# One level of Strassen's method for the gate and up products of four feed-forward blocks

## The chip, the cores and the metric

The kernel runs on one core of a Trainium2 chip. The metric is the device time of one execution in microseconds; the median of several executions counts. In what follows PE is the matrix engine, DVE the vector engine, ACT the scalar engine, POOL the engine GpSimd, and SP the queue that issues the transfers.

## The reference, cut to what matters

The model is one inference step of a two-layer decoder trunk over 512 prompt tokens and 64 sample tokens (576 columns together) of width 1024. Each layer has a feed-forward block ahead of its token mixer and another behind its cross attention, so there are four such blocks in all. The hidden width `D_FF` is 2816.

```python
def swiglu(x, w_gu, w_down):
    gate, up = jnp.split(x @ w_gu, 2, axis=-1)
    return (jax.nn.silu(gate) * up) @ w_down

for l in range(DEPTH):
    x = x + 0.5 * swiglu(rmsnorm(x, ffn1_norm[l]), ffn1_w_gu[l], ffn1_w_down[l])
    # token mixer, cross attention
    x = x + 0.5 * swiglu(rmsnorm(x, ffn2_norm[l]), ffn2_w_gu[l], ffn2_w_down[l])
```

All data are 32-bit floats.

## The kernel before, in words

Activations lie transposed: 128 rows of the width on the partitions, the 576 tokens along the free axis, eight such chunks `xT[:, c]`. A product in full precision is made of three products in the faster format fp32r: each operand is split into a rounded high part `h` and a remainder `l`, and PE adds up hh, hl and lh. ACT makes `h` (a cast), DVE makes `l` (a subtraction).

`unit` (line 273) loads 256 columns of a weight, all 1024 rows, as one transfer of 1 MB into a `raw` buffer (two of them), and splits it in two halves of 128x1024 each into `wh` and `wl` (three buffers each; the cast is line 297, the subtraction line 298). `mm3` (line 302) makes 128 rows of the result: 8 chunks of the width, times 3 products, times 2 halves of 288 tokens, which is 48 matmuls of 288 columns into a pair of PSUM banks `psd` (two pairs). So a unit of 256 weight columns takes 96 matmuls.

`ffn` (line 402) walks the 22 hidden chunks in three parts of 8, 8 and 6 chunks. In each part it goes by two chunks at a time: a gate unit and an up unit. DVE multiplies the gate's PSUM by the norm's factor `rstd` (line 420), ACT takes Silu (line 421), DVE multiplies the up's PSUM by `rstd` (line 424) and then by the gate (line 425), and `split` makes the two parts of the hidden chunk (lines 318 and 319). At the end of a part the down product runs over the part's hidden chunks for all eight output chunks, and `add_x` (line 1392) adds each to `xT`. In the last part `nxt` follows each output chunk: `norm_chunk` (line 323) makes the next block's split input `xn` from one chunk of `xT` (lines 333 and 334) and adds its squares to `acc` (lines 348 and 350, on POOL). `norm_finish` (line 397) sums `acc` over the partitions with PE (line 388) and makes `rstd`.

The program is written for a framework that sets all waits itself and that fixes, before the run, the order of the instructions of each engine from the order of the code, the dependencies and the free buffers. On the chip each engine takes its instructions strictly in that order. Tags with a number of buffers hold the chunks: `x0` and `x1` (pairs), `y`, `m`, `g0`, `g1`, `t0`, `t1`.

Of the kernel before, what the change touches and what calls it, by code (L numbers as in the profile page):

```python
# [140 lines left out]
class Net:  # L141
    def __init__(self, ctx, tc, a, o):
        self.tc, self.nc, self.a, self.o = tc, tc.nc, a, o
        sb = lambda n, b: ctx.enter_context(tc.tile_pool(name=n, bufs=b))
        self.cp = sb("const", 1)
        self.wp = sb("weights", 2)
        self.kp = sb("chunks", 1)
        self.sp = sb("small", 4)
        self.dp = ctx.enter_context(tc.tile_pool(name="dram", bufs=1, space=bass.MemoryType.DRAM))
        self.pd = ctx.enter_context(tc.tile_pool(name="pd", bufs=2, space=bass.MemoryType.PSUM))  # L150
        self.pm = ctx.enter_context(tc.tile_pool(name="pm", bufs=4, space=bass.MemoryType.PSUM))
        self.bufs = dict(y=8, m=11, g0=6, g1=6, t0=3, t1=3)
        self.n = 0
        self.tmp = 't'
        self.lane = 0
# [10 lines left out]
    def ct2(self, lane, dt=F32):  # L166
        return self.kp.tile([P, 2, T], dt, tag=f"x{lane}", bufs=4, name=self.nm("x"))

    def tt(self):
        return self.ct(self.tmp)  # L170
# [8 lines left out]

    def psm(self):  # L180
        return self.pm.tile([P, 512], F32, tag=f"m{self.lane}", bufs=2, name=self.nm("pm"))

# [88 lines left out]

    # -- dense products ---------------------------------------------------
    def unit(self, *srcs, ksplit=False):
# [28 lines left out]
    def mm3(self, w, xin):  # L302
# [11 lines left out]
        return ps[:, :, :TH]  # L314

    def split(self, x, tag='y'):
        h, l = self.ct(tag, F32R), self.ct(tag, F32R)
# [5 lines left out]
    def norm_chunk(self, c, name, base, squares=True):  # L323
# [6 lines left out]
        if name != 'final_norm':  # L330
            t = self.ct2(c % 2, F32R)
# [68 lines left out]

    # -- feed forward -----------------------------------------------------
    def ffn(self, l, which, nxt, begin=None, then=None):
        nc = self.nc
        gu, dn = self.a[f'ffn{which}_w_gu'][l], self.a[f'ffn{which}_w_down'][l]
        units = lambda m0: [self.unit(gu[:, c * P:(c + 2) * P]) for c in (m0, KF + m0)]
        first = units(0)
        if begin:
            begin()
        self.norm_finish()
        xn, rstd = self.xn, self.v2(self.rstd)  # L410
        self.tmp = 'g'
        parts = [(0, 8), (8, 16), (16, 22)]
        for pi, (c0, c1) in enumerate(parts):
            hid = []
            for m0 in range(c0, c1, 2):
                ug, uu = units(m0) if m0 else first
                for j in range(2):
                    pg = self.mm3(ug[j], xn)
                    z = self.tt()
                    nc.vector.tensor_mul(self.v2(z), pg, rstd)  # L420
                    nc.scalar.activation(z, z, AF.Silu)
                    pu = self.mm3(uu[j], xn)
                    h = self.tt()
                    nc.vector.tensor_mul(self.v2(h), pu, rstd)  # L424
                    nc.vector.tensor_mul(h, h, z)
                    hid.append(self.split(h, 'y' if len(hid) < 4 else 'm'))
                if then and m0 == 2:
                    then()
# [7 lines left out]

    # -- even mixer -------------------------------------------------------
    def col_scale(self, ps):
# [157 lines left out]
    def even_mixer(self, filler, nxt):  # L596
# [22 lines left out]
        def proj(h):  # L619
            self.lane = h % 2  # L620
            uf, uq = self.unit(col(4, h), col(3, h))
            _, t = self.half_tanh(self.mm3(uf, xn))
            f, k = self.ct('m'), self.ct('m')
            nc.vector.tensor_scalar(f, t, c1[:, h:h + 1], c0[:, h:h + 1], ALU.mult, ALU.add)
# [73 lines left out]

    # -- odd mixer: retention ---------------------------------------------
    def rope(self, ps):  # L700
# [6 lines left out]
        out = self.ct('m')  # L707
        nc.vector.tensor_add(out, t, sw)
        return out
# [25 lines left out]

    # -- odd mixer: delta rule --------------------------------------------
    def shift_mix(self, ps, ci, dst):
# [25 lines left out]
    def prep(self, j, w_in):  # L763
        col = lambda g: w_in[:, 2048 + g * 512 + j * P:2048 + g * 512 + (j + 1) * P]
        ur, uk = self.unit(col(0), col(1))
        uv, = self.unit(col(2))
        tag = 'g' if j < 2 else 'm'
        r, kd, v = self.ct(tag), self.ct(tag), self.ct('m')
        for ci, u, t in ((j, ur, r), (4 + j, uk, kd), (8 + j, uv, v)):
# [311 lines left out]
    def odd_mixer(self, filler, nxt):  # L1081
# [20 lines left out]
        def proj(h):  # L1102
            uq, uk = self.unit(col(0, h), col(1, h))
            q = self.rope(self.mm3(uq, xn))
            k = self.rope(self.mm3(uk, xn))
            uv, ug = self.unit(col(2, h), col(3, h))
# [66 lines left out]

    # -- cross attention --------------------------------------------------
    def mem_stats(self):
# [14 lines left out]

    def wkv(self, l, tag):
        nc, a, o = self.nc, self.a, self.o
# [3 lines left out]
        for c in range(0, KD, 4):  # L1196
# [5 lines left out]
            for k in range(4):  # L1202
                if k % 2 == 0:
                    h, lo = self.ct(tag, F32R), self.ct(tag, F32R)
                ks, g = slice(k % 2 * MEM, (k % 2 + 1) * MEM), self.vec('mem_norm', l * KD + c + k)
# [76 lines left out]
    def xattn(self, l, nxt):  # L1282
# [8 lines left out]
        for m0 in range(0, KD, 2):  # L1291
            u = self.unit(a['xattn_wq'][l][:, m0 * P:(m0 + 2) * P])
            for j in range(2):
                t = self.ct('g')
                nc.vector.tensor_mul(self.v2(t), self.mm3(u[j], self.xn), self.v2(rs))
                nc.gpsimd.tensor_copy(qs[:, m0 + j], t[:, TP:])
                q.append([self.ct('y' if m0 < 4 else 'm', F32R)[:, :TP] for _ in range(2)])
                self.split_to(*q[-1], t[:, :TP])
# [9 lines left out]
        def prompt_head(h):  # L1308
# [17 lines left out]
            for d in range(2):  # L1326
                c = 2 * h + d
                ps = self.psm()
                for m in range(2):
                    for i, k in pairs:  # L1330
                        nc.tensor.matmul(ps, v[m][i][:, c // 4, c % 4 * P:(c % 4 + 1) * P], pT[m][k],  # L1331
                                         start=(m + i + k == 0), stop=(m == 1 and i == 1))
                tag = 'y' if h in (1, 2) else 'm'
                out[c] = self.ct(tag, F32R), self.ct('g1' if c == 1 else tag, F32R)
                self.split_to(*(t[:, :TP] for t in out[c]), ps)
# [90 lines left out]
def network(tc, a, o):  # L1426
    with ExitStack() as ctx:
# [3 lines left out]
        n.ffn(0, 1, after('mix_norm', 0), lambda: n.norm_all('ffn1_norm', 0), n.setup_rest)  # L1431
        n.even_mixer(lambda: n.wkv(0, 'y'), after('xattn_norm', 0))
        n.xattn(0, after('ffn2_norm', 0))
        n.ffn(0, 2, after('ffn1_norm', 1))
        n.ffn(1, 1, after('mix_norm', 1))
        n.odd_mixer(lambda: n.wkv(1, 'y'), after('xattn_norm', 1))
        n.xattn(1, after('ffn2_norm', 1))
        n.ffn(1, 2, after('final_norm', 0))
# [16 lines left out]
```

## Time and profile before

| what | us |
|---|---|
| median of 3 runs | 3076.28 |
| lowest and highest run | 3063.57, 3079.44 |
| span of the profiled execution | 3078.6 |
| PE busy in that span | 3002.7 |
| DVE, ACT, POOL busy in that span | 1480.8, 1006.3, 273.6 |

For the profiled execution no device time is listed beside its span; the span of 3078.6 us runs from its first to its last instruction and lies within the range of the timed runs, 2.3 us over their median. The three runs lie 16 us apart. Busy times are times in which the engine had an instruction in work; that PE is busy for 98% of the span does not say yet that each matmul is needed, only that it hardly waits.

### The profile page before, as it was taken

To read this page: it belongs to the slowest core of one execution; us is meant where nothing else is said; L and a number is where in the kernel's file an instruction comes from. 1 tells how busy PE (TensorE), PEld (TensorE's weight loads), DVE (VectorE), ACT (ScalarE), POOL (GpSimd) and SP (SyncE) were. 2 spreads that over 40 slices of the span, in tenths; PEclk is the share of its full clock that TensorE was granted. 3 is DMA by queue.
4 is the path that set the end of the run, shared out by engine and by line. 5 is a ranking of instruction groups with operands and counts; after the bars stand their busy time and mean duration, and the time that the engine had idled before them with its cause. 6 is when DMAs were issued, how large, how long until landed. Compare 5 with 4: busy or idle time off the path is not lost.

```text
span 3078.6 us, 52891 instructions
## 1 busy us (share of the span) xinstructions
PE 3002.7 (98%) x23236; PEld 2849.9 (93%) x23236; DVE 1480.8 (48%) x2271; ACT 1006.3 (33%) x1495; POOL 273.6 (9%) x299
## 2 busy tenths in 40 slices
PE   8999999999999999999999999999989999999998
PEld 7999999998978999999999999988767788999998
DVE  4434346555545433334434345466576545433333
ACT  4322242222534322224212134433253434322223
POOL 0000011111101000001000001123222100000001
PEclk9999999999999999999999999999889999999999
DMA  4222222222445222222222223322113244222221
GB/s 136 96 84 83 84 77 70 70 84 91 146 174 170 72 84 84 84 80 80 83 83 83 83 83 89 86 63 67 39 43 84 83 162 168 83 83 83 83 79 62
DMA packets 295869, 278.63 MB, mean 91 GB/s; under 512 B 25028, under 2 KB 278808, under 8 KB 295640
## 3 DMA queue, kind: packets, MB, share of 16 engines
q1 hardware_dynamic: 295640, 275.26, 28.2%
q8 instruction: 183, 3.00, 0.4%
q14 instruction: 46, 0.38, 0.0%
HBM read 262.09 MB, written 13.14 MB: 89 GB/s over the span
## 4 chain that ended last, share of the span: by engine, by line
PE 89%; ACT 3%; DVE 3%; issue 2%; POOL 1%; DMA 1%; SPq 0%; ACTq 0%; POOLq 0%; DVEq 0%
PE pd L311 74%; PE pm L833 2%; PE pm L757 1%; PE pd L1222 1%; PE pm L388 1%; PE pd L1253 1%; PE pd L1221 1%; PE pd L1223 1%; PE pm L527 1%; PE pm L1347 1%; PE pm L1315 1%; PE pm L1331 1%; POOL acc L350 1%; PE pm L566 1%; PE pm L942 1%
## 5 line engine op out<-in xcount | busy, mean ns | idle before, releaser
L311 PE MATMUL pd<-x,wh 128*128 128x288 f32 x8000 | 1415.4, 298 | 4.5 <-ACT wh L297 4.3
L311 PEld LDWEIGHTS pd<-x,wh 128*128 128x128 f32 x8000 | 1188.7, 190 | 10.6 <-ACT wh L297 5.4
L311 PE MATMUL pd<-x,wl 128*128 128x288 f32 x4000 | 867.1, 298 | 0.0
L297 ACT CAST wh<-raw 128x1024 fp32r<-128x1024 f32 (+1 forms) x378 | 389.6, 1031 | 1346.9 <-PE pd L311 1252.4
L311 PEld LDWEIGHTS pd<-x,wl 128*128 128x128 f32 x4000 | 649.5, 190 | 2.5 <-DVE wl L298 0.3
L298 DVE TENSOR_TENSOR wl<-raw,wh 128x1024 fp32r<-128x1024 f32 (+1 forms) x378 | 454.9, 1204 | 32.4 <-ACT wh L297 6.8
L311 PE MATMUL pd<-y,wh 128*128 128x288 f32 x2304 | 415.6, 300 | 1.1 <-ACT y L318 0.8
L311 PEld LDWEIGHTS pd<-y,wh 128*128 128x128 f32 x2304 | 343.7, 190 | 5.4 <-ACT y L318 1.1
L1392 DVE SCALAR_TENSOR_TENSOR xT<-pd,xT 128x576 f32<-128x576 f32 x144 | 108.8, 756 | 402.1 <-PE pd L311 402.1
L311 PE MATMUL pd<-m,wh 128*128 128x288 f32 x1504 | 264.0, 296 | 0.3 <-ACT m L1279 0.3
L311 PE MATMUL pd<-y,wl 128*128 128x288 f32 x1152 | 251.6, 299 | 0.0
L424 DVE TENSOR_TENSOR g<-pd,rstd 128x576 f32<-128x576 f32 x88 | 66.6, 756 | 374.6 <-PE pd L311 374.6
L311 PEld LDWEIGHTS pd<-m,wh 128*128 128x128 f32 x1504 | 222.1, 189 | 0.8 <-ACT m L1279 0.8
L311 PEld LDWEIGHTS pd<-y,wl 128*128 128x128 f32 x1152 | 187.7, 190 | 1.4
L350 POOL TENSOR_TENSOR acc<-acc,g 128x576 f32<-128x576 f32 x27 | 41.8, 1550 | 1602.4 <-ACT g L348 1258.1
L311 PE MATMUL pd<-m,wl 128*128 128x288 f32 x768 | 164.4, 296 | 0.0
L420 DVE TENSOR_TENSOR g<-pd,rstd 128x576 f32<-128x576 f32 x88 | 66.6, 756 | 196.2 <-PE pd L311 196.0
L311 PEld LDWEIGHTS pd<-m,wl 128*128 128x128 f32 x768 | 123.8, 189 | 0.0
L1222 PE MATMUL pd<-wh,y 128*128 128x256 f32 x256 | 77.6, 303 | 0.0
L1223 PE MATMUL pd<-wl,y 128*128 128x256 f32 x256 | 77.3, 302 | 0.0
L1221 PE MATMUL pd<-wh,y 128*128 128x256 f32 x256 | 76.3, 298 | 0.6 <-DVE y L1207 0.6
L287 ACT CAST wh<-raw 128x1024 fp32r<-128x1024 f32 x32 | 33.5, 1046 | 121.6 <-PE pd L1222 60.9
(461 smaller groups left out, 2946.3 us busy)
## 6 DMA issues: line engine op xcount, KB each, us to landing
raw<-ffn_w_gu SPq DMA_DIRECT2D x88, 1024.0 KB
raw<-ffn_w_down SPq DMA_DIRECT2D x32, 1024.0 KB
raw<-xattn_wkv SPq DMA_DIRECT2D x16, 1024.0 KB
x<-cache_mem_v SPq DMA_DIRECT2D x32, 512.0 KB
raw<-cache_mem_k SPq DMA_DIRECT2D x16, 1024.0 KB
raw<-odd_w_in SPq DMA_DIRECT2D x30, 512.0 KB
raw<-ffn_w_down SPq DMA_DIRECT2D x16, 768.0 KB
raw<-even_w_in SPq DMA_DIRECT2D x16, 512.0 KB
```

The source lines that it names most:

```text
L287: nc.scalar.copy(h, raw[:, k:k + nk // 2])
L297: nc.scalar.copy(h, raw[:, :, c:c + step])
L298: nc.vector.tensor_sub(l, raw[:, :, c:c + step], h.bitcast(F32))
L311: nc.tensor.matmul(ps[:, hf, :TH], w[:, k], x[:, hf * TH:(hf + 1) * TH], start=(k == 0 and w is wh and xi == 0), stop=(k == nk - 1 and w i ...
L350: eng.tensor_add(self.acc, self.acc, sq)
L420: nc.vector.tensor_mul(self.v2(z), pg, rstd)
L424: nc.vector.tensor_mul(self.v2(h), pu, rstd)
L833: self.nc.tensor.matmul(ps[q, c * 64:(c + 1) * 64], *fn(c, q))
L1221: nc.tensor.matmul(ps[:, m, :256], mh[:, ms], wh, start=(k == 0), stop=False)
L1222: nc.tensor.matmul(ps[:, m, :256], ml[:, ms], wh, start=False, stop=False)
L1223: nc.tensor.matmul(ps[:, m, :256], mh[:, ms], wl, start=False, stop=(k == KD - 1))
L1392: self.nc.vector.scalar_tensor_tensor(x, ps, s, x, ALU.mult, ALU.add)
```

## The change

The gate and up products are made with Strassen's method in the form with seven products. The weight's 1024 rows are taken as two sets (even and odd chunks), its 256 columns as two halves, and the 576 tokens as two halves of 288. Each of the seven products has a combination of weight blocks and a combination of token blocks as its operands, 4 chunks of the width and 3 products of fp32r, so 12 matmuls of 288 columns; seven of them replace the 96 matmuls of a unit by 84.

The combinations of the weight blocks are made on POOL, in place in `raw`: four additions or subtractions of 128x512 for each unit. Each of the seven forms is split by one cast on ACT and one subtraction on DVE of 128x512. The seven results are combined as they leave PSUM: a copy and two additions of 128x288 on DVE (`p1`, `u2`, `u3`), and then one `put` for each quarter of the result. For the gate, three quarters are a DVE addition and a POOL multiplication by `rstd` and one is a DVE multiplication; after Silu, POOL multiplies by `rstd` again for the up product. For the up product, three quarters are a DVE addition and a DVE multiplication and one is a DVE multiplication.

The token blocks' seven combinations are made ahead, in `token_forms`, once for each pair of chunks as the block before delivers it. The parts become 6, 6, 6 and 4 hidden chunks. `y` becomes six pair buffers, which the forms T4, B21 and B22 hold through a block; `m` has 7 buffers in place of 11, and users of `y` and `m` elsewhere are adapted.

```diff
-        self.bufs = dict(y=8, m=11, g0=6, g1=6, t0=3, t1=3)
+        self.bufs = dict(m=7, g0=6, g1=6, t0=3, t1=3)
...
+    def pair(self, dt=F32):
+        return self.kp.tile([P, 2, T], dt, tag="y", bufs=6, name=self.nm("y"))
...
+    def form(self, src, n):
+        nc = self.nc
+        nj = src.shape[1]
+        t = self.wp.tile([P, 1024], F32R, tag=("wh", "wl")[n % 2], bufs=3, name=self.nm("wf"))
+        h, l = (t[:, i * nj * P:(i + 1) * nj * P].rearrange("p (j f) -> p j f", j=nj) for i in range(2))
+        nc.scalar.copy(h, src)
+        nc.vector.tensor_sub(l, src, h.bitcast(F32))
+        return h, l
+
+    def unit_forms(self, *srcs):
...
+        v = raw.rearrange("p (j two) f -> p two j f", two=2)
+        a11, a12, a21, a22 = v[:, 0, :, :P], v[:, 1, :, :P], v[:, 0, :, P:], v[:, 1, :, P:]
+        s3 = self.ct('t1')[:, :nk * 64].rearrange("p (j f) -> p j f", f=P)
+        nc.gpsimd.tensor_sub(s3, a21, a11)
+        nc.gpsimd.tensor_add(a21, a21, a22)
+        yield self.form(a11, 0)
+        nc.gpsimd.tensor_sub(a11, a21, a11)
+        yield self.form(a11, 1)
+        yield self.form(s3, 0)
+        yield self.form(a21, 1)
+        nc.gpsimd.tensor_sub(a11, a12, a11)
+        yield self.form(a22, 0)
+        yield self.form(a11, 1)
+        yield self.form(a12, 0)
...
+    def seven(self, forms, x, put):
+        nc = self.nc
+        w = lambda: next(forms)
+        ps = self.psd()
+        a, d = ps[:, 0, :TH], ps[:, 1, :TH]
+        s, s_ = self.v2(self.ct('t0')), self.ct('t0')
+        p1, u2, u3 = s[:, 0], s[:, 1], s_[:, :TH]
+        self.product(a, w(), x['B11'])
+        nc.vector.tensor_copy(p1, a)
+        b = self.psm(0)[:, :TH]
+        self.product(b, w(), x['T2'])
+        nc.vector.tensor_add(u2, b, p1)
+        c = self.psm(1)[:, :TH]
+        self.product(c, w(), x['T3'])
+        nc.vector.tensor_add(u3, c, u2)
+        self.product(d, w(), x['T1'])
+        put(1, 1, d, u3)
+        e = self.psm(0)[:, :TH]
+        self.product(e, w(), x['T4'])
+        put(1, 0, e, u3)
+        self.product(d, w(), x['B22'], True)
+        self.product(a, w(), x['B21'], True)
+        put(0, 1, d, u2)
+        put(0, 0, a, None)
...
+        nc.vector.tensor_sub(t1, x12, x11)
+        put('B11', x11, g1)
+        nc.scalar.activation(t1, t1, AF.Identity, scale=g1)
+        nc.vector.scalar_tensor_tensor(t2, x22, g2, t1, ALU.mult, ALU.subtract)
+        put('T2', t2, None)
+        nc.vector.scalar_tensor_tensor(t3, x11, g1, t2, ALU.mult, ALU.subtract)
+        put('T3', t3, None)
+        put('T1', t1, None)
+        nc.vector.scalar_tensor_tensor(t4, x21, g2, t2, ALU.mult, ALU.subtract)
...
-        parts = [(0, 8), (8, 16), (16, 22)]
+        parts = [(0, 6), (6, 12), (12, 18), (18, 22)]
...
+                    if u is None:
+                        nc.vector.tensor_mul(zv[n][:, t], ps, r[:, t])
+                    else:
+                        nc.vector.tensor_add(zv[n][:, t], ps, u)
+                        nc.gpsimd.tensor_mul(zv[n][:, t], zv[n][:, t], r[:, t])
...
+                for t in z:
+                    nc.scalar.activation(t, t, AF.Silu)
+                    nc.gpsimd.tensor_mul(t, t, self.rstd)
...
+                    if u is None:
+                        nc.vector.tensor_mul(hv[n][:, t], ps, zv[n][:, t])
+                    else:
+                        nc.vector.tensor_add(hv[n][:, t], ps, u)
+                        nc.vector.tensor_mul(hv[n][:, t], hv[n][:, t], zv[n][:, t])
```

## Rows read from the trace of the kernel before

**Rows 1.** The page: span, and the engines' busy time, share and instructions.
```profile
span 3078.6 us, 52891 instructions
PE 3002.7 (98%) x23236; PEld 2849.9 (93%) x23236; DVE 1480.8 (48%) x2271; ACT 1006.3 (33%) x1495; POOL 273.6 (9%) x299
```
**Rows 2.** Stretches: a block, cross attention, the second mixer; columns in the first row.
```profile
core 0: us, PE busy (x) PEld busy (x) DVE busy (x) ACT busy (x) POOL busy (x), PEclk, DMA share, GB/s
1443.50:1860.00 416.50, 416.50 (x3127) 416.50 (x3126) 168.02 (x188) 111.07 (x130) 7.50 (x5) 1.00 0.25 82
833.00:1018.00 185.00, 178.00 (x1382) 154.49 (x1382) 95.36 (x180) 78.18 (x159) 20.02 (x24) 1.00 0.45 153
```
**Rows 3.** Timeline of a gate chunk: start, duration, instruction, idle time before and its releaser.
```profile
181.40 1.05 ACT L297 CAST wh<-raw 128x1024 fp32r<-128x1024 f32 x1 [5.35 <-PE pd L311]
...
182.48 1.23 DVE L298 TENSOR_TENSOR wl<-raw,wh 128x1024 fp32r<-128x1024 f32 x1
...
188.06 0.76 DVE L420 TENSOR_TENSOR g<-pd,rstd 128x576 f32<-128x576 f32 x1 [4.35 <-PE pd L311]
```
**Rows 4.** Groups by form, DVE and ACT: count, busy us, mean ns, idle before.
```profile
L1280 DVE TENSOR_TENSOR m<-g,m 128x512 fp32r<-128x512 f32 x8 | 5.5, 689 | 5.9 <-ACT m L1279 5.9
L1078 DVE TENSOR_TENSOR m<-x,pm 128x288 f32<-128x288 f32 x8 | 3.3, 449 | 0.1
L561 DVE TENSOR_TENSOR g<-m,g 128x288 f32<-128x288 f32 x8 | 3.6, 452 | 0.1
L319 DVE TENSOR_TENSOR m<-g,m 128x576 fp32r<-128x576 f32 x40 | 30.3, 758 | 29.7 <-ACT m L318 29.7
L1279 ACT CAST m<-g 128x512 fp32r<-128x512 f32 x8 | 5.0, 619 | 19.4 <-DVE g L1295 19.4
L421 ACT ACTIVATE g<-g 128x576 f32<-128x576 f32 x88 | 60.5, 687 | 3.2 <-DVE g L420 2.9
```
**Rows 5.** Timeline of DVE alone: two instructions back to back.
```profile
2092.29 0.75 DVE L801 TENSOR_TENSOR g<-g,g 128x576 f32<-128x576 f32 x1
2092.96 0.75 DVE L803 SCALAR_TENSOR_TENSOR g<-t,g 128x576 f32<-128x576 f32 x1
```
**Rows 6.** Timeline, DVE and POOL at the same time, both reading two operands in SBUF.
```profile
1426.03 1.42 POOL L350 TENSOR_TENSOR acc<-acc,g 128x576 f32<-128x576 f32 x1 [3.38 <-ACT g L348]
...
2063.50 1.44 POOL L806 TENSOR_TENSOR t<-t,t 128x576 f32<-128x576 f32 x1 [2.03 <-DVE t L805]
...
2063.93 2.10 DVE L298 TENSOR_TENSOR wl<-raw,wh 128x1024 fp32r<-128x1024 f32 x1
...
2096.85 1.21 DVE L298 TENSOR_TENSOR wl<-raw,wh 128x1024 fp32r<-128x1024 f32 x1
2096.88 2.43 POOL L806 TENSOR_TENSOR t<-t,t 128x576 f32<-128x576 f32 x1
...
2099.28 1.40 POOL L814 TENSOR_TENSOR g<-g,t 128x256 f32<-128x256 f32 x2
```
**Rows 7.** Timeline: POOL beside a DVE instruction that reads one operand in PSUM.
```profile
817.99 1.43 POOL L350 TENSOR_TENSOR acc<-acc,t 128x576 f32<-128x576 f32 x1 [1.44 <-ACT t L348]
...
818.90 0.76 DVE L1392 SCALAR_TENSOR_TENSOR xT<-pd,xT 128x576 f32<-128x576 f32 x1 [0.78 <-PE pd L311]
```
**Rows 8.** Timeline: the end of the third block's input and its norm.
```profile
1438.14 0.76 DVE L1392 SCALAR_TENSOR_TENSOR xT<-pd,xT 128x576 f32<-128x576 f32 x1 [1.97 <-PE pd L311]
...
1440.43 1.78 POOL L350 TENSOR_TENSOR acc<-acc,g 128x576 f32<-128x576 f32 x1 [2.98 <-ACT g L348]
1442.27 1.24 PE L388 MATMUL pm<-acc,cblob 128*128 128x288 f32 x4 [1.23 <-POOL acc L350]
```
**Rows 9.** Timeline: the start of the program, inputs of the first block.
```profile
14.73 3.73 DVE L334 SCALAR_TENSOR_TENSOR x<-xT,vecn,x 128x576 fp32r<-128x576 f32 x5 [0.24 <-ACT x L333]
...
40.40 0.77 PE L311 MATMUL pd<-x,wh 128*128 128x288 f32 x4 [0.19 <-DVE g L420]
```

More of the change, by code (lines that the diff above doesn't have):

```diff
@@ L167, in ct2, with two @@
         return self.kp.tile([P, 2, T], dt, tag=f"x{lane}", bufs=4, name=self.nm("x"))
+    def pair(self, dt=F32):
+        return self.kp.tile([P, 2, T], dt, tag="y", bufs=6, name=self.nm("y"))
+    def two(self, paired, dt=F32R):
+        if not paired:
+            return self.ct('m', dt), self.ct('m', dt)
+        t = self.pair(dt)
+        return t[:, 0], t[:, 1]
     def tt(self):
@@ new lines, in product @@
+    def product(self, ps, w, x, more=False):
+        (wh, wl), (xh, xl) = w, x
+        n = wh.shape[1]
+        for j in range(n):
+            for i, (a, b) in enumerate(((wh, xh), (wh, xl), (wl, xh))):
+                self.nc.tensor.matmul(ps, a[:, j], b[:, j], start=(not more and j + i == 0),
+                                      stop=(j == n - 1 and i == 2), skip_group_check=more)
+    def seven(self, forms, x, put):
+        nc = self.nc
+        w = lambda: next(forms)
[20 more added lines that the diff above has]
+        put(0, 0, a, None)
@@ L320, in split, with norm_chunk @@
         return h, l
-    def norm_chunk(self, c, name, base, squares=True):
+    def norm_chunk(self, c, name, base, squares=True, late=False):
         nc = self.nc
@@ L415, in ffn, with gate, up @@
             for m0 in range(c0, c1, 2):
[L416 to L426, printed above, removed]
+                z = [self.ct('g') for _ in range(2)]
+                zv = [self.v2(t) for t in z]
+                def gate(n, t, ps, u):
+                    if u is None:
+                        nc.vector.tensor_mul(zv[n][:, t], ps, r[:, t])
+                    else:
+                        nc.vector.tensor_add(zv[n][:, t], ps, u)
+                        nc.gpsimd.tensor_mul(zv[n][:, t], zv[n][:, t], r[:, t])
+                self.seven(self.unit_forms(gu[:, m0 * P:(m0 + 2) * P]), x, gate)
+                for t in z:
+                    nc.scalar.activation(t, t, AF.Silu)
+                    nc.gpsimd.tensor_mul(t, t, self.rstd)
+                h = [self.ct('g') for _ in range(2)]
+                hv = [self.v2(t) for t in h]
+                def up(n, t, ps, u):
+                    if u is None:
+                        nc.vector.tensor_mul(hv[n][:, t], ps, zv[n][:, t])
+                    else:
+                        nc.vector.tensor_add(hv[n][:, t], ps, u)
+                        nc.vector.tensor_mul(hv[n][:, t], hv[n][:, t], zv[n][:, t])
+                self.seven(self.unit_forms(gu[:, (KF + m0) * P:(KF + m0 + 2) * P]), x, up)
+                for t in h:
+                    hid.append(self.split(t, 'm' if len(hid) < 3 else 'g1'))
                 if then and m0 == 2:
@@ L1296, in xattn @@
                 nc.gpsimd.tensor_copy(qs[:, m0 + j], t[:, TP:])
-                q.append([self.ct('y' if m0 < 4 else 'm', F32R)[:, :TP] for _ in range(2)])
+                q.append([x[:, :TP] for x in self.two(m0 < 6)])
                 self.split_to(*q[-1], t[:, :TP])
```

88 lines of the change are left out of this document (66 added, 22 removed).

## The prediction

> **What bounds the kernel now.** I read the page first, then stretches by stage, then the timeline of one gate chunk. The page says that PE is busy for 3002.7 of 3078.6 us [rows 1]. The stretches tell where the rest is: inside a feed-forward block PE is busy for all of 416.50 us at full granted clock (1.00, the 2.4 GHz level), while DVE works for 168.02 us, ACT for 111.07 and POOL for 7.50; in cross attention PE misses 7 us of 185 [rows 2]. So within a block time is the number of matmuls times their spacing: 416.50 us by 3127 matmuls is 0.1332 us each [rows 2]. The timeline shows how the other engines follow: ACT and DVE sit idle for 4 to 5 us until PE frees a buffer or ends a chunk, then work one or two instructions [rows 3]. Nothing but PE is late. Work taken off PE there comes off the time, as long as the others keep up, and the change gives all three of them more.
>
> **What it removes.** A unit of 256 gate or up columns goes from 96 matmuls to 84 of the same form, 288 columns. There are 88 units (4 blocks, 11 pairs of a gate and an up unit). 88 x 12 x 0.1332 is 140.7 us. The PE time of a pair falls from 192 x 0.1332 = 25.6 to 168 x 0.1332 = 22.4 us. The down products keep their 1056 matmuls for a block.
>
> **What a pair now costs on DVE.** Durations: a 128x512 subtraction 0.69 us, a 128x288 operation 0.45 with or without PSUM, a 128x576 split 0.76 [rows 4]. Back to back, instructions start 0.08 us closer than they last (0.67 for one of 0.75 [rows 5]), so I count 0.61, 0.37 and 0.68. Fourteen subtractions are 8.5 us; six for p1, u2, u3, four for the gate's quarters and seven for the up's are 17 x 0.37 = 6.3; two splits 1.4. Sum 16.2 of 22.4 us, 6.9 in the gate unit and 9.3 in the up unit, against 11.2 us of PE for each. ACT has 14 casts at 0.62, two Silu at 0.69 and two splits as long, 11.4 us: it hides.
>
> **POOL, and what it shares with DVE.** Alone, a POOL operation on two full operands takes 1.42 us for 576 columns and 0.70 for 256 [rows 6]; between them lie 1.28 for 512 and 0.77 for 288. A pair has eight of 512, three of 288 and two of 576: 10.2 + 2.3 + 2.8 = 15.3 us. That alone fits into 22.4. But when POOL and DVE both read two SBUF operands, they don't overlap: the DVE subtraction of 1.21 us took 2.10 beside POOL, and POOL's 1.42 became 2.43 beside the same subtraction [rows 6]. Each such meeting costs the later one what is left of the earlier, less some 0.15 us. A DVE operation with one operand in PSUM is free of it: 0.76 beside POOL, and POOL kept its 1.43 [rows 7].
>
> Of the pair's DVE work, 14 subtractions, three multiplications of 288 and two splits read two SBUF operands: 8.5 + 1.1 + 1.4 = 11.0 us. With POOL's 15.3 that is 26.3 us of exclusive work for 22.4 us of PE. Thirteen POOL operations with 0.15 us of grace at both ends give back up to 3.9: 22.4 to 26.3 us for a pair. On average it just fits.
>
> It won't fit evenly. In the up unit DVE has 9.3 us and meets four POOL operations of 512 and two of 576. One of 512 holds DVE up by at most 1.28 - 0.37 (a PSUM operation beside it) - 0.15 = 0.76, one of 576 by 0.90: at most 4.8, say 3, so 12.3 for 11.2 us. The gate unit has 6.9 and at most 3.9, say 2, and catches up. What DVE may be late by is set by bank d: product 6 adds into it, so the quarter (1,1) must have left it within product 5, 12 x 0.133 = 1.6 us, less 0.37 for the addition itself, 1.2 us. Lateness beyond that stops PE. Nothing in the trace shows it; I take 1 us for each of the 28 up units that aren't the last of a part, 28 us. In the last one of a part DVE prepares down weights, four subtractions in place of seven, and POOL no next unit, so it gets nothing.
>
> Bounds of this term: 0, and the exclusive sum throughout. Six forms and one raw buffer can be prepared under the down product before a part (six subtractions 3.7, POOL 5.1, less 3.5 us that the down weights put into the last unit), 5.3 us credit for each part. (26.3 - 22.4) x 3 - 5.3 = 6.4 us in 12 parts and (3.9 x 2) - 5.3 = 2.5 in 4: 87 us.
>
> **A rule of the Trainium skill.** It says in GPSIMD Engine Reference, section "Key points", that GpSimd shares its SBUF interfaces with VectorE and contends with instructions that have two SBUF inputs, and in "Engine selection" it sends elementwise work to VectorE. The 2.10 and 2.43 us agree with the first. By the second, the 13 operations would go to DVE: 16.2 + 8 x 0.61 + 3 x 0.37 + 2 x 0.68 is 23.6 us for a pair, over PE's 22.4 and under the exclusive 26.3, so by it this change has put them on the wrong engine.
>
> **Lateness by order.** Each engine keeps its fixed order, so a subtraction that waits for POOL's combination holds up the evacuations behind it on DVE, and PE behind those. Before, POOL had no part in a block [rows 2]; no row prices it. Ends: 0, and one 128x512 subtraction (0.61) for each of 88 units, 54 us. Forms are up to six products (9.6 us) ahead, so I take near the lower end, 0.1 us each: 9 us.
>
> **Starts of the blocks.** Token forms take 11 DVE operations of 288 for two chunks (4.1 us) where two of 576 did before. Block 3 follows block 2 directly: its last down part has 4 chunks, so two output chunks take 48 x 0.133 = 6.4 us, and DVE has 4.1 + two `add_x` 1.4 + a 1024 subtraction 1.15 = 6.7 and meets two POOL squares of 1.42 us. Late by 0 to 2 us, four times: I take 7 us. Behind cross attention two output chunks take 12.8 us and hide it; the chain from the last `add_x` over t1, t2 and their splits (some 3 us) and the late forms cost 2 us each, twice, by the like of the 1.23 us that PE waits there already [rows 8]. At the start of the program DVE makes 44 operations (16 us) where eight took 6.5, but PE stood mostly idle until rstd was there at 40 us anyway [rows 9]: 4 us. Sum 15, ends 0 and 30.
>
> **What hides.** 32 `add_x` in place of 24 in a block, 0.76 us each under 4.8 us of a down chunk. A transfer of 1 MB every 11.2 instead of 12.8 us, 94 GB/s where 82 run, and 153 run elsewhere [rows 2]. Fewer `m` and paired `y` buffers in the mixers: 0, within 5 us either way, since buffers that hold the same chunks come to the same count (8 + 11 before, 12 + 7 after).
>
> **The sum.** 140.7 - 28 - 9 - 15 = 89 us, so 3078.6 becomes 2990 in span. The span lies 2.3 us over the median, so the median goes from 3076.3 to 2987 us.
>
> **Rivals.** (1) Everything hides but the starts: -140.7 + 15, 2951 us. For it: on average the exclusive work just fits. Against it: the up unit's uneven load. (2) The shared access binds and running ahead doesn't help, because what is late is the evacuation and not the forms: 44 pairs at 26.3, 3.9 x 44 = 172, + 9 + 15 - 140.7 = +55, 3131 us, slower. It decides from a pair of 22.4 + (140.7 - 24)/44 = 25.1 us on. For it: the 2.10 and 2.43 us [rows 6]. Against it: the grace of 0.15 us and the DVE operations in PSUM that run beside POOL [rows 7]. (3) The matmuls fall in number but not in time: groups of 12 in changing banks space out. At 0.143 us in place of 0.1332, 7392 x 0.0098 = 72 us go, 3060 us. Against it: where one chunk's 48 end and the next begin, no gap stands (PE busy 416.50 of 416.50 [rows 2]).
>
> **How the numbers follow.** Forecast 0.57, rival 1 0.20, rival 2 0.16, rival 3 0.07. The range runs from 2945 (just under rival 1) to 3090: all the costs at their upper ends, 87 + 54 + 30 = 171, would give 3107, which I leave out with most of rival 2. A measurement of this kernel can tell 0.5%, some 15 us, from no change. Slower by that: most of rival 2, 0.13. Within it: the rest of that, half of rival 3 and a tail of the forecast, 0.10. Faster: 0.77.
>
> **What would show it.** Spacing: matmuls in a block stay at 0.133 us and number 1056 fewer. POOL busy some 44 x 15 us more, and more than that if it meets DVE; subtractions of 128x512 with a mean over 0.69 us. PE's idle time before products 6, released by DVE's `put`, mostly in up units. Idle of PE in the blocks of about 50 us in all. I am wrong if PE waits for casts or POOL rather than for evacuations, if the granted clock falls below 1.00 in the blocks, or if the mixers' stretches move by more than 10 us.

## The result, and the profile after

The changed kernel takes 3252.6 us (median; 3244.7 to 3263.6) against 3077.9 for the kernel before on the same chip: 1.058 of the time, 95% interval 1.055 to 1.061. The forecast was 2987 us with a range of 2945 to 3090. It is wrong in sign, and by 266 us. Of the rivals the second, at 3131 us, had the right sign and less than a third of the size.

First the page of after: span, busy times, the granted clock by slices, and the chain that ended last.

```profile
span 3261.8 us, 53788 instructions
PE 2968.7 (91%) x22180; PEld 2782.6 (85%) x22180; DVE 2096.7 (64%) x3387; ACT 1192.0 (37%) x2046; POOL 1030.0 (32%) x871
PEclk8899999999999999999999999999889799999999
PE 56%; DVE 16%; POOL 12%; ACT 6%; issue 5%; DMA 5%; SPq 0%; ACTq 0%; DVEq 0%; POOLq 0%
```

Against [rows 1], the 1056 matmuls are gone (23236 to 22180), but PE is no longer busy all the time (98% to 91%), and no other engine comes near being full: DVE has 64%, POOL 32%. An engine that is full would be a bound that a sum of busy times can find. Here there is none, and the chain, which a kernel bound by PE would spend on PE, spends 39% of its time on DVE, POOL, ACT and transfers.

By stages, cut at the first matmul of each norm, in the profiled executions (us):

| stage | before | after | difference |
|---|---|---|---|
| start of the program | 32.8 | 45.0 | +12.2 |
| feed-forward blocks 1, 2, 3, 4 | 421.8, 424.8, 424.8, 423.8 | 467.5, 469.2, 455.7, 455.5 | +152.6 |
| the two mixers | 381.2, 592.5 | 375.5, 609.8 | +11.6 |
| cross attention, twice | 181.7, 181.6 | 184.5, 185.5 | +6.7 |

So the loss is in the four blocks, the very place where 140.7 us were to come off. (The second mixer's 609.8 us stands against 589 to 601 us in eleven of the twelve kernels below, with the same code there as after, so I don't count it as an effect of the change.) Block 3 of after, and in it a stretch as long as one part; columns as in [rows 2]:

```profile
1541.70:1997.30 455.60, 411.20 (x2908) 403.35 (x2908) 306.82 (x439) 155.63 (x247) 193.00 (x145) 0.96 0.25 81
1667.00:1752.00 85.00, 74.76 (x506) 73.12 (x506) 63.13 (x95) 29.15 (x50) 42.52 (x33) 0.92 0.23 74
```

A part holds three pairs of a gate and an up unit; I measure it from the first matmul of its units to the first of its down products. At PE's spacing it is 3 x 22.4 = 67.2 us; it lasts 85.0, so 28.3 us a pair. In such a stretch PE is idle for 10 us, and what it does is stretched to 74.8 us at a granted clock of 0.92. Yet DVE is busy for 63 of the 85 us, POOL for 43, ACT for 29. Every engine waits.

What they wait for over the whole program, in the waits of after (us in total, times, longest):

```profile
POOL t L351 <- DMA raw<-ffn_w_gu: 439.5, 44, 28.0
POOL raw L354 <- DVE wf L337: 430.4, 83, 8.5
ACT wf L336 <- POOL raw L354: 285.6, 87, 4.6
ACT g L558 <- POOL g L554: 243.0, 88, 4.0
DVE wf L337 <- ACT wf L336: 236.4, 190, 4.0
PE pd L368 <- DVE t L379: 142.9, 68, 3.7
```

POOL waits for DVE, ACT for POOL, DVE for ACT, and POOL for a transfer. That can be a ring. The sums alone don't prove it, since an engine with nothing to do waits too. In thin, a kernel of the next section that leaves POOL nearly idle, two of these waits are as large or larger, and PE runs at its floor all the same:

```profile
POOL raw L354 <- DVE wf L337: 587.9, 85, 12.7
POOL t L351 <- DMA raw<-ffn_w_gu: 444.9, 52, 31.7
```

The transfer's 439.5 us of after are mostly outside the parts, too: fourteen waits of 14 us and more make up 357 of them, while within a part one lasts 2 to 3 us. So I followed single instructions. The chain of waits through one round of it (start, length, what), from one POOL combination of line 354 to the same one a pair later:

```profile
1671.86 1.30 POOL raw L354
1673.18 0.63 ACT wf L336
1673.84 0.70 DVE wf L337
1674.61 1.67 POOL raw L358
1676.28 1.71 POOL t L351
1678.06 1.63 POOL raw L352
1679.68 0.78 POOL g L554
1680.48 0.70 ACT g L558
1681.24 1.40 POOL g L559
1682.64 1.21 POOL g L554
...
1684.47 0.61 ACT wf L336
1685.10 1.51 DVE wf L337
...
1686.66 5.68 DMA raw<-ffn_w_gu
1692.41 1.28 POOL t L351
1693.69 1.47 POOL raw L358
1695.19 0.63 ACT wf L336
1695.84 1.12 DVE wf L337
1696.96 0.37 DVE g L567
...
1702.63 1.29 POOL raw L354
```

From 1671.86 to 1702.63 is 30.8 us for one pair, and the next round takes 29.7. I add up the pieces, those left out included: POOL 12.5, DVE 8.2, the transfer 5.7, ACT 2.6, hand-overs 1.9. PE isn't in it. The links: line 354 overwrites in place a quarter that DVE's subtraction has just read; ACT casts what POOL made; DVE subtracts; POOL goes through its queue in order, with the next unit's combinations ahead of this unit's multiplications by rstd; ACT takes Silu before its next cast, and Silu waits for POOL; DVE's last subtraction sets the raw buffer free; the transfer fills it; POOL can go on. A round of 30 us against PE's 22.4 is why PE stands still. A pair takes 28.3 us and not 30 (85.0/3); I put that down to the forms that are made ahead before a part begins (3 x 30 less 85.0 is some 5 us).

The groups of after that answer to [rows 4], [rows 6] and [rows 7] (count, busy us, mean ns, idle before):

```profile
L337 DVE TENSOR_TENSOR wf<-raw,wf 128x512 fp32r<-128x512 f32 x528 | 494.7, 951 | 273.8 <-ACT wf L336 236.4 <-POOL raw L352 35.7
L337 DVE TENSOR_TENSOR wf<-t,wf 128x512 fp32r<-128x512 f32 x88 | 108.3, 1231 | 0.0
L568 DVE TENSOR_TENSOR g<-g,g 128x288 f32<-128x288 f32 x132 | 111.0, 841 | 5.1
L351 POOL TENSOR_TENSOR t<-raw 128x512 f32<-128x512 f32 x88 | 134.3, 1527 | 439.5 <-DMA raw<-ffn_w_gu 439.5
L352 POOL TENSOR_TENSOR raw<-raw 128x512 f32<-128x512 f32 x88 | 126.2, 1434 | 4.1
L354 POOL TENSOR_TENSOR raw<-raw 128x512 f32<-128x512 f32 x88 | 114.2, 1298 | 430.5 <-DVE wf L337 430.4
L358 POOL TENSOR_TENSOR raw<-raw 128x512 f32<-128x512 f32 x88 | 144.2, 1638 | 45.9 <-DVE wf L337 45.9
```

The subtraction that takes 0.69 us alone [rows 4] takes 0.95 and 1.23 here, and the multiplication of 288 columns 0.84 instead of 0.45. That agrees with the shared access of [rows 6]. So two costs are mixed in this trace: the collisions, and the ring. The experiments had to part them.

### The profile page after: what moved, and what is told of

It is laid out like the page before. It is cut to its first block, busy times and chain, and to the rows that moved or that the text cites. A ratio compares the mean times of both kernels' runs of the same rounds, so it can differ in the third digit from the quotient of the medians.

```text
span 3261.8 us, 53788 instructions
## 1 busy us (share of the span) xinstructions
PE 2968.7 (91%) x22180; PEld 2782.6 (85%) x22180; DVE 2096.7 (64%) x3387; ACT 1192.0 (37%) x2046; POOL 1030.0 (32%) x871
## 3 DMA queue, kind: packets, MB, share of 16 engines
q1 hardware_dynamic: 295896, 275.26, 26.3%
## 4 chain that ended last, share of the span: by engine, by line
PE 56%; DVE 16%; POOL 12%; ACT 6%; issue 5%; DMA 5%; SPq 0%; ACTq 0%; DVEq 0%; POOLq 0%
PE pd L321 34%; DVE wf L337 6%; PE pd L368 4%; DMA raw<-ffn_w_gu 4%; POOL raw L358 3%; ACT wf L336 3%; PE pm L368 3%; POOL t L351 2%; POOL g L554 2%; POOL raw L354 2%; PE pm L980 2%; PE pm L903 1%; PE pm L520 1%; PE pd L1402 1%; PE pd L1371 1%
## 5 line engine op out<-in xcount | busy, mean ns | idle before, releaser
L337 DVE TENSOR_TENSOR wf<-raw,wf 128x512 fp32r<-128x512 f32 x528 | 494.7, 951 | 273.8 <-ACT wf L336 236.4
L368 PE MATMUL pd<-x,wf 128*128 128x288 f32 x2112 | 355.3, 321 | 171.9 <-DVE t L379 142.9
L336 ACT CAST wf<-raw 128x512 fp32r<-128x512 f32 x528 | 308.8, 615 | 544.4 <-POOL raw L354 285.6
L368 PEld LDWEIGHTS pd<-x,wf 128*128 128x128 f32 x2112 | 321.1, 207 | 190.9 <-DVE t L379 156.3
L321 PE MATMUL pd<-x,wh 128*128 128x288 f32 x2368 | 433.1, 302 | 0.0
L321 PEld LDWEIGHTS pd<-x,wh 128*128 128x128 f32 x2368 | 356.5, 191 | 5.6 <-ACT wh L307 0.9
L368 PE MATMUL pm<-x,wf 128*128 128x288 f32 x2112 | 308.6, 300 | 18.9 <-ACT x L415 8.2
L368 PE MATMUL pd<-y,wf 128*128 128x288 f32 x2112 | 300.4, 297 | 24.1 <-DVE g L567 16.1
L351 POOL TENSOR_TENSOR t<-raw 128x512 f32<-128x512 f32 x88 | 134.3, 1527 | 439.5 <-DMA raw<-ffn_w_gu 439.5
L321 PE MATMUL pd<-x,wl 128*128 128x288 f32 x1184 | 262.0, 302 | 0.0
L321 PEld LDWEIGHTS pd<-x,wl 128*128 128x128 f32 x1184 | 194.0, 191 | 1.9
```

Source lines behind the costliest of these rows:

```text
L321: nc.tensor.matmul(ps[:, hf, :TH], w[:, k], x[:, hf * TH:(hf + 1) * TH], start=(k == 0 and w is wh and xi == 0), stop=(k == nk - 1 and w i ...
L336: nc.scalar.copy(h, src)
L337: nc.vector.tensor_sub(l, src, h.bitcast(F32))
L351: nc.gpsimd.tensor_sub(s3, a21, a11)
L368: self.nc.tensor.matmul(ps, a[:, j], b[:, j], start=(not more and j + i == 0), stop=(j == n - 1 and i == 2), skip_group_check=more)
```

## The experiments

Four theories. **E**, evacuation: PE waits for DVE's copy out of PSUM (line 379), as the trace says, since products a and d share one PSUM tile. **S**, shared access: DVE's work is stretched by POOL until DVE is the bound (rival 2). **C**, the chain or ring through POOL: its latency sets the pace, with or without collisions. **H**, head of the queue: POOL stands waiting for a transfer with work behind it. The recorded expectations have letters of their own: A is E throughout, B is the ring, and C is the shared access in dvec and thin, POOL's lengths alone in thin_r, and the ring in alldve and fast. Ratios are to the kernel before, with 95% intervals.

**banks** gives product d a PSUM tile of its own, so that it no longer waits for the copy of a (E).

```diff
-        ps = self.psd()
-        a, d = ps[:, 0, :TH], ps[:, 1, :TH]
+        a, d = self.psd()[:, 0, :TH], self.psm(1)[:, :TH]
...
-        c = self.psm(1)[:, :TH]
+        c = self.psm(0)[:, :TH]
```

> The changed kernel with one edit: product a and product d no longer share one PSUM tile (d gets its own, c moves to the other small bank). In the trace of the changed kernel PE waited 143 us for the copy p1 before product d. Theory A (evacuation: PE is stopped because a read of one half of the PSUM pair holds up the write of the other): that wait goes and nothing takes its place, 3253 us becomes 3110 to 3150 us. Theory B (preparation: the chain raw weights, POOL combination, ACT cast, DVE subtraction, release of raw, transfer, POOL sets 28.4 us for a pair): the wait only moves to another place, 3230 to 3260 us.

3231.9 us, ratio 1.049 (1.045 to 1.052): 21 of 175 us. In its waits, PE's wait for line 379 is gone, and one for the next DVE instruction, line 381, stands in its place with nearly the same sum:

```profile
PE pm L368 <- DVE t L381: 136.1, 66, 3.6
```

E falls. The wait that the trace puts on PE is the last link of a chain that is late as a whole; take the link away and the next one is as late.

**dvec** moves the four weight combinations of each unit (lines 351, 352, 354 and 358) from POOL to DVE.

> The changed kernel with the four weight combinations of each unit on DVE instead of POOL; POOL keeps the five multiplications by rstd. Theory C (shared SBUF access: DVE and POOL lengthen each other): the 128x512 subtractions fall from 0.95 us back to about 0.70, DVE has 21 us of work in a pair of 22.4 us of PE, a pair takes 23 to 24.5 us, 3030 to 3090 us. Theory B (order and length of the preparation chain, of which the sharing is a part): the combinations take 0.69 instead of 1.28 to 1.64 us but now queue behind the evacuations, a pair takes 25 to 26.5 us, 3110 to 3170 us. Theory A: no gain or a loss, 3240 us or more.

3086.6 us, ratio 1.002 (1.000 to 1.004): 166 us back, by giving DVE *more* to do. The time lies in the range expected from the shared access. As the move takes away collisions and links of the ring together, it doesn't part the two.

**thin** leaves POOL's instructions of the gate and up units in place but cuts them to 32 and 16 columns, and takes the third form from a12: most of the combinations and of the multiplications by rstd is not computed. **thin_r** cuts only the multiplications by rstd.

> The changed kernel with POOL's operations in the gate and up stage kept in number and place but cut to a few columns (32 of 512 for the weight combinations, 16 of 288 or 576 for the multiplications by rstd); the rest of the combinations and multiplications is left out, and the third form reads a raw block. POOL then holds nobody up for more than some 0.2 us. Theories B and C both: a pair falls to 22.4 to 23.5 us, 2960 to 3030 us in all. If transfers that come late, or the fixed order alone, set the pace: over 3100 us. Theory A: 3150 us or more, since DVE keeps its evacuations.

> The changed kernel with only the multiplications by rstd on POOL cut to 16 columns (the rest of them is left out); the weight combinations stay whole. It takes a third of POOL's time off (5.1 of 15.3 us in a pair). Theory B (ACT stands in Silu until POOL has multiplied, and the casts stand behind Silu): the wait of Silu for POOL, 243 us in all, goes, and the casts of forms 6 and 7 come 1.5 to 3 us earlier: a pair falls by 2 to 4 us, 3080 to 3165 us. Theory C by lengths alone: a third of the excess of 6 us for a pair, 2 us, 3165 us. Theory A: under 30 us gain.

thin: 2982.6 us, 0.967 (0.963 to 0.970). thin_r: 3150.8 us, 1.022 (1.019 to 1.025). With POOL nearly empty the change gives 95 us; the rest of the loss, 270 us, is POOL's, and its multiplications by rstd alone account for 102 of them. A part of block 3 lasts 67.2 us in thin, which is PE's floor to the tenth.

**beside and solo** part collisions and ring. beside leaves out POOL's real work (and takes the third form from a12, as thin does), and lets POOL add nearly as much, 693 us for after's 766, into a tile that nobody reads: collisions without a ring. solo leaves the ring as it is, and gives each POOL instruction a constant as its second operand: a ring without collisions.

```diff
 beside:
         nc.scalar.copy(h, src)
+        if beside:
+            nc.gpsimd.tensor_add(self.dum, h.bitcast(F32), h.bitcast(F32))
         nc.vector.tensor_sub(l, src, h.bitcast(F32))
 solo:
-        nc.gpsimd.tensor_sub(s3, a21, a11)
-        nc.gpsimd.tensor_add(a21, a21, a22)
+        nc.gpsimd.tensor_scalar_mul(s3, a21, 0.9)
+        nc.gpsimd.tensor_scalar_mul(a21, a22, 0.9)
...
```

> The shared access by itself. The four combinations and the multiplications by rstd are left out (the output isn't the reference's), and the third form is taken from a12; instead POOL does, beside six of the seven forms of each unit, one 128x512 addition of two SBUF operands into a scratch tile that nobody reads: about 15 us a pair, as much as POOL's real work. Nothing waits for these additions, apart from the release of the form that they read. Control: the kernel with POOL's instructions cut to a few columns, 2982.6 us. If the loss of the change comes from the chain (who waits for POOL), this stays at 2980 to 3040 us. If the collisions of DVE and POOL lengthen DVE's work until it is the bound, DVE's 16.2 us a pair become 24 to 27 and the time is 3080 to 3200 us, most of the loss without a single consumer of POOL.

> The chain by itself. Every POOL instruction of the gate and up units stays in its place, with the same waits and readers, but has one SBUF operand and a constant (a multiplication by 0.9) in place of two SBUF operands, so that the output isn't the reference's; in the trace of after an instruction of this kind and size took 1.49 us (128x512, line 675) beside 1.30 to 1.64 for the real ones. The rows of before show DVE and POOL in each other's way only where both read two SBUF operands, so the collisions should be gone and the subtraction of line 337 back at 0.7 us (0.95 in after). With the kernel whose POOL work was cut to a few columns (2982.6), the one with POOL work that nobody reads (3060.9) and after (3252.6) this makes a table of four. If chain and collisions simply add, it comes out near 3170 us (3130 to 3210). If POOL's place in the chain costs only because the collisions stretch it, it stays at 2985 to 3060 us.

| | no collisions | collisions |
|---|---|---|
| no ring | thin 2982.6 | beside 3060.9 (+78) |
| ring | solo 3185.6 (+203) | after 3252.6 (+270) |

beside has a ratio of 0.996 (0.994 to 0.997), solo 1.035 (1.033 to 1.036). solo came out as expected for costs that add; beside lies between its two ranges, so collisions cost more than the ring's theory had for them, and less than S wants. The two costs alone add up to 281 us, together they are 270. Block 3 of beside, then of solo:

```profile
1447.71:1857.06 409.35, 396.04 (x2907) 391.81 (x2907) 302.85 (x438) 161.37 (x245) 179.24 (x135) 0.99 0.28 90
```

```profile
1508.16:1950.84 442.68, 403.33 (x2908) 395.20 (x2909) 253.59 (x439) 155.31 (x247) 206.81 (x145) 0.98 0.26 83
```

The reader should compare DVE's column (the third busy time) with the length. In beside DVE is busy for 302.9 us, nearly after's 306.8, and the block is 46 us shorter than after's. In solo DVE has 253.6, some 53 less than after, and the block is only 13 us shorter. So the length of the block doesn't follow DVE's busy time, as S wants it; it is long where the ring is. How the two groups stand, in beside and in solo:

```profile
L338 POOL TENSOR_TENSOR t<-wf 128x512 f32<-128x512 f32 x528 | 692.8, 1312 | 883.0 <-ACT wf L336 856.0
L339 DVE TENSOR_TENSOR wf<-raw,wf 128x512 fp32r<-128x512 f32 x616 | 603.8, 989 | 62.7 <-ACT wf L336 62.7
```

```profile
L337 DVE TENSOR_TENSOR wf<-raw,wf 128x512 fp32r<-128x512 f32 x528 | 369.8, 714 | 417.5 <-ACT wf L336 417.5
L354 POOL TENSOR_SCALAR raw<-raw 128x512 f32<-128x512 f32 x88 | 132.2, 1503 | 373.6 <-DVE wf L337 373.5
```

In beside the subtraction is stretched to 0.99 us, as in after; in solo it is back at 0.71, with POOL as busy. So [rows 6] held where both sides have two SBUF operands, and with one on POOL's side most collisions are gone. Two reserves: solo's POOL instructions last somewhat longer than the real ones (its six groups sum to 823 us, after's to 766), and 43 of its 616 subtractions still last 0.85 us or more, all beside POOL. So its 203 us may be a little high.

**porder** puts the next unit's first combination, which waits for a transfer, behind this unit's last one in POOL's queue (H).

> The changed kernel, with one thing different: the next unit's first combination (line 351), which waits for a transfer, is put into POOL's queue only after this unit's last combination (line 358). If the stand at the head of POOL's queue (440 us of POOL's idle time is put down to that transfer) is what costs, the last combination is no longer late and the time falls by 50 to 150 us, to 3100 to 3200 us. If POOL's length and the collisions cost, and the stand only fills time in which POOL would be late anyway, it stays within 30 us of 3252.6 us, or grows since the next unit's combinations then start later.

3239.1 us, ratio 1.054 (1.052 to 1.056), 13 us under after, with intervals that just overlap; a part of block 3 lasts 84.8 us against 85.0. H falls, although 439.5 us of waiting stand in after's trace against that transfer. What is left of them here (line 352 is after's 351) stands at the ends of parts and the starts of blocks:

```profile
POOL t L352 <- DMA raw<-ffn_w_gu: 384.6, 18, 28.6
```

Within a part POOL doesn't wait for a transfer any more, and the chain of one round (1700.46 to 1729.93, 29.5 us) has no transfer in it: DVE's own queue has 13.7 us of it, POOL 7.5, ACT 2.5. So the transfer of the chain above is one of two paths of about equal length, and taking it away gives nothing.

**first2 and last2** move two combinations each to DVE: lines 351 and 352, or lines 354 and 358.

> Only the first two of the four weight combinations (lines 351 and 352), which wait for nothing but the transfer, go from POOL to DVE. If it is the amount of POOL work that counts, this lies halfway between after (3252.6) and the kernel with all four on DVE (3086.6), near 3170 us, and within 30 us of the kernel that moves the other two. If the chain counts (POOL between a subtraction of DVE and a cast of ACT), these two are the harmless ones and moving them gives less: 3180 to 3240 us.

> Only the last two combinations (lines 354 and 358) go from POOL to DVE. Both overwrite a quarter that DVE's subtraction of line 337 has just read, and ACT's next cast waits for them (285.6 and 109.7 us of ACT's idle time are put down to them). If the chain counts, this gives most of what moving all four gives: 3090 to 3150 us. If the amount counts, near 3170 us and within 30 us of the kernel that moves the first two.

3159.2 us (1.027; 1.025 to 1.028) and 3153.1 us (1.025; 1.024 to 1.027), within 6 us of each other; halfway between after and dvec is 3170. My notion that the first two are harmless, since they wait only for a transfer, was wrong. Both times are those that the other expectation gave, by the amount of POOL's work. The amount by itself isn't it, since beside has 693 us of POOL's work that nobody reads and costs 78 us; it must be the amount that stands in the ring. The chain above suggests why the first two count as much: POOL's order sets them (1676.28 and 1678.06) ahead of the multiplication that Silu waits for, so the ring passes through them too. This explanation came after the runs, and no run tests it.

**alldve and fast.** alldve moves all 13 POOL operations of a pair to DVE. fast has besides the tiles of banks, and p1 copied by ACT (`nc.scalar.copy(p1, a)`).

> All POOL work of the gate and up units goes to DVE: the four weight combinations and the multiplications by rstd. By the rows of before DVE then has about 23.6 us of work a pair (gate unit and up unit) against TensorE's 22.4. Theory C (the chain through POOL: each unit's forms wait for POOL's combinations, which stand in one queue with the multiplications by rstd and wait there for transfers and for the shared access): no POOL instruction and no collision is left, so a pair costs 23 to 24.5 us and the time is 2980 to 3060 us. Theory S (DVE simply has too much to do, with or without POOL): DVE gets still more work than in the kernel with the combinations alone on DVE (3086.6 us), so 3090 to 3200 us.

> As alldve, and two things more: product d gets a PSUM tile of its own, and the copy of product a out of PSUM (p1) goes to ACT, which takes about 0.7 us a pair from DVE. Theory C: DVE has 22.9 us a pair against TensorE's 22.4, so TensorE is the bound again or nearly so: 2960 to 3030 us, below the kernel before. Theory S: 3060 us or more. If the evacuation out of PSUM has a share of its own once POOL is gone, fast lies more than 30 us below alldve; if it has none, they lie within 30 us.

alldve: 3018.7 us, ratio 0.983 (0.979 to 0.986). fast: 3014.8 us, 0.981 (0.978 to 0.984). Both are faster than both kernels: 57 and 61 us than before, by 234 and 238 than after. The evacuation has no share that can be told (4 us apart). A part of block 3 lasts 68.4 us in alldve and 67.2 in fast from the second part on: PE's floor again. The rest against thin (32 us) stands in the first part of the blocks (in block 3 74.4 us in fast, 67.4 in thin): each of the four is 7 to 8 us longer than in thin. Block 3 of alldve:

```profile
1425.94:1829.77 403.83, 397.95 (x2917) 392.42 (x2917) 323.88 (x581) 159.05 (x250) 11.31 (x7) 0.99 0.28 91
```

DVE is busy for 323.9 of 403.8 us there and does everything. In after it is busy for 306.8, with POOL working 193 us for it. On the page DVE has 2149.9 us in alldve and 2096.7 in after. The six groups that POOL did take 368 us on DVE (60.3 + 60.4 + 62.9 + 60.3 + 66.2 + 58.1); giving them to POOL took only 53 us off it. Of the difference 239 us came back as longer subtractions (line 337, 603.0 us for 415.6) and multiplications (line 568, 111.0 for 59.5); the rest I put down to DVE's back-to-back instructions, which overlap [rows 5], so that a group adds up more than the page counts.

**slack** is fast with one thing given back to POOL, the multiplication of line 559, which stands in no ring that I see.

> The kernel with all gate and up work on DVE, a bank of its own for product d and p1 on ACT (0.981 of before), with one thing given back to POOL: the multiplication of the gate's result by rstd (line 559), two a pair. It stands in no ring: it waits for Silu, and the up unit reads it only after its fourth product, some 7 us later. It takes 1.5 us a pair from DVE (66 us in all). Theory of the ring with collisions counted apart: 88 POOL instructions that nobody waits for cost what the 528 unread ones cost, 78/528 = 0.15 us each, 13 us in all, against up to 66 us of DVE's work: ratio 0.970 to 0.981, 2985 to 3018 us. If any POOL work with two SBUF operands costs what moving the multiplications by rstd from POOL to DVE gave (68 us for 220 instructions, 0.31 us each), this loses 27 us: ratio 0.987 to 0.993.

3051.5 us, ratio 0.991 (0.988 to 0.994): 1% slower than fast, by 37 us for 88 instructions. The second expectation held. So the 0.15 us apiece of beside don't carry over; I put that down to DVE having had time to lose there, which no run shows. The groups of slack (line 558 is after's 559):

```profile
L558 POOL TENSOR_TENSOR g<-g,rstd 128x576 f32<-128x576 f32 x88 | 148.9, 1695 | 1318.5 <-ACT g L557 1318.5
L351 DVE TENSOR_TENSOR t<-raw 128x512 f32<-128x512 f32 x88 | 88.1, 1001 | 9.9 <-DMA raw<-ffn_w_gu 9.8
L358 DVE TENSOR_TENSOR raw<-raw 128x512 f32<-128x512 f32 x88 | 79.8, 906 | 0.5
```

In fast the DVE groups of lines 337, 351, 352, 354, 358 and 553 sum to 720 us, here to 820: the 88 POOL instructions cost DVE 100 us, more than the 66 they took from it. One meeting in slack's timeline:

```profile
1786.36 1.77 POOL L558 TENSOR_TENSOR g<-g,rstd 128x576 f32<-128x576 f32 x1 [55.94 <-ACT g L557]
...
1786.76 1.92 DVE L358 TENSOR_TENSOR raw<-raw 128x512 f32<-128x512 f32 x1
```

The combination takes 0.69 us alone; beside POOL it starts 0.4 us behind and ends 0.55 us after POOL does.

So the length of the ring is shown by the trace, and its cost by solo. That the raw buffers are one of its links rests on the chain alone, and porder speaks against a cost of theirs. A third raw buffer was not tried.

## Why the prediction was wrong

**The bound before, and what was removed: right.** Without POOL's load a part takes 67.2 us, 3 x 22.4, as the spacing of 0.1332 us has it.

**Lateness by order: the step that failed.** I wrote "Forms are up to six products (9.6 us) ahead, so I take near the lower end, 0.1 us each: 9 us", with ends of 0 and 54. solo measures 203, nearly four times the upper end. The upper end came from one subtraction for each unit, so from a single wait; I didn't follow the waits round until they closed. Nearly all I needed stood in the diff and in the rows: in-place combinations, Silu between two casts on ACT, two raw buffers, and the durations of [rows 4]; the transfer's 5.7 us did not. With POOL's 1.28 us for a combination and DVE undisturbed, the same pieces still sum to some 28 us: POOL 10.6 (six combinations, two multiplications of 0.77, one of 1.42), DVE 6.9, and transfer, ACT and hand-overs as above. solo, with nearly no collisions, takes 27.3 (82.0/3). The sums by engine, on which the forecast stands, can't show this: they say what an engine can do when it never waits.

**Running ahead** was the excuse for it. Six forms of reserve are a stock. A ring of 30 us a pair against 22.4 uses up 7.6 us of it with every pair, so 9.6 us last for little more than one of a part's three pairs.

**POOL and the shared access: mechanism right, size and place off.** The exclusive access of [rows 6], DVE's freedom with an operand in PSUM [rows 7], 1.28 us for a combination alone (1.30 at line 354, where DVE waits) all held. The term was 28 us with ends of 0 and 87; beside measures 78. POOL's real work is 17.4 us a pair (2 x (1.53 + 1.43 + 1.30 + 1.64) + 3 x 0.92 + 2 x 1.43) instead of 15.3, since it is stretched too. The place is right in one point: in beside PE's largest wait is for a gate addition before product 6 (line 551, 45.6 us in all). But I had looked for it in up units, and had called the gate unit the one that catches up.

**Rival 2** got the sign by this term alone: 26.3 us a pair, while a pair took 28.3 (85.0/3). That was luck: the collisions alone take a pair to 23.6 us (70.7/3 in beside), and evacuations don't set the pace either, as banks gave 21 us. The ring, which it left at 9 us, makes up most of the loss.

**By the Trainium skill's rule**, GPSIMD Engine Reference, "Engine selection", elementwise work belongs on VectorE; I had worked out 23.6 us a pair by it. alldve agrees with the rule and takes 22.8 (68.4/3).

**Starts: 15 us with ends of 0 and 30, too small.** In thin the program's start is 40.1 us instead of 32.8, where I gave 4. The blocks, which should each be 35.2 us shorter, are 406.8, 401.2, 393.5 and 391.3 us: 20, 11, 4 and 3 too long. Together some 45 us. Block 1 of thin shows part of it as a granted clock of 0.98 and one wait of 5.5 us; the rest I haven't followed up.

**What hides: as forecast, as far as the runs show.** The transfers are no bound by rate (94 GB/s were expected, 81 ran). One of them stands in the chain with 5.7 us, but porder takes it out and is no faster within a part. `add_x` and the mixers' buffers did hide: the first mixer is 5.7 us shorter.

**The signs to look for** were right in part. Of those that were to show an error, the clock fell below 1.00 in the blocks (0.96), and the second mixer moved by 17.3 us in the profile, though by less than 10 in eleven of the twelve other kernels. Idle time of PE, forecast at about 50 us in the four blocks together, is 43 to 55 in each. But PE hardly waits for casts, the sign that I named first, although casts were late: in its waits

```profile
PE pd L368 <- DVE t L379: 142.9, 68, 3.7
PE pd L368 <- DVE g L567: 16.1, 21, 1.5
PE pd L368 <- ACT wf L336: 14.7, 5, 7.5
```

an evacuation leads, which I had named as the mark of being right. It isn't even the one foreseen, the wait before product 6 for a `put` (lines 553 and 567, 23 us together), but that of product 4 for the copy of line 379, and banks shows that it costs little.

## What to carry to other kernels

Where a change puts a second engine between two others, follow the waits from an instruction round to the same instruction one iteration later, with each engine's order, each overwrite in place and each buffer's release, and compare that round with the bound; sums of busy times see nothing of it. An elementwise operation with two SBUF operands is not off DVE when it is given to POOL: while POOL has it DVE's own such operations stand still (the subtraction of 1.92 us above). In no pair of kernels here did it pay. A wait in the trace names who came last, not what is late: one of the largest here was taken away for 21 us, and another, POOL's 439.5 us for a transfer, stands in thin with 444.9 and costs nothing there.

## What the runs showed of the hardware

**In slack POOL costs DVE more than it saves.** 88 POOL multiplications of 1.70 us cost DVE 100 us; on DVE they take 66, 0.75 us for one (slack and fast).

**One SBUF operand and a constant on POOL is nearly free of collisions** (DVE's subtraction 0.71 us in solo, 0.69 in thin; for the third form's 88 it is 0.78), but no shorter for POOL: 1.50 us for 128x512, where two operands take 1.28 undisturbed.

**The granted clock is lower in the blocks where PE waits.** In block 3 it is 1.00, the 2.4 GHz level, in the kernel before and in thin, 0.99 in beside, 0.98 in solo and 0.96 in after, and 0.92 within a part of after (means between the two levels). It doesn't follow the waiting alone: fast has 0.98 with only 4 us of idle time in block 3, solo the same with 39; the same 2908 matmuls are busy for 390.5 us in thin and for 411.2 in after. As the ring sets the pace there, I don't count this as a cost of its own. No run parts the two.
